# An encoder block in exact fp32 by halves: the gate projection's first products interleaved, tiles placed in another order, filler matmuls dealt out anew

## The chip, the cores and the metric

The kernel runs on one core of a Trainium2 chip. The metric is the device time of one execution in microseconds (us), the median over runs. A second figure, the span, is the length of one profiled execution as the hardware profiler shows it; that execution also has a time of its own.

## The reference

One layer of a hybrid bidirectional encoder: 1024 tokens, model width 1024, everything in float32.

```
h = RMSNorm(x)
q,k,v,r, lr_f,lr_b, sq,sk,sv, gate_a,gate_b = split(h @ W_in)
A = bidirectional gated linear attention(q,k,v; gates from lr_f, lr_b), 4 heads,
    chunked, per-head RMSNorm, times silu(r), then @ W_oA
B = windowed attention (+-128 tokens, blocks of 128), 8 query heads, 2 key heads,
    QK-norm, rotary positions, a sink logit per head, then @ W_oB
x = x + (sigmoid(gate_a) * A + sigmoid(gate_b) * B) @ W_out
x = x + SwiGLU(RMSNorm(x))
```

## The kernel before, in words

Every large product works on 128x128 blocks of weights against 128x512 blocks of activations. A float32 operand is split into a high part in TensorE's reduced float32 format (ScalarE's copy, `h`) and the remainder (VectorE's subtraction, `l`); a product is the sum of three matmuls, high x high, high x low and low x high. `wunit` is the helper for a weight block of 128x512: a load on the SP queue into `wr`, the split into `wh` (L70) and `wl` (L72). A result stays in a PSUM bank (`mmtile`, four banks, or `chtile`, four more) until ScalarE or VectorE copies it out.

The kernel goes through these stages.

1. Head of the kernel: x is loaded in blocks `xr[k, s]` (k = 0 to 7 blocks of 128 features, s = 0, 1 halves of the tokens), split, and used for the first head's q and k and for the low-rank gate codes `lr`.
2. The branch gates `gate_a`, `gate_b`, eight pairs f = 0 to 7. Each pair is computed with seven block products instead of eight (a Strassen-like scheme on 2x2 blocks: features in two halves, tokens in two halves). `x_first(f)` does the first two of the seven: one product into a bank, ScalarE's copy `p1` out of it (L320), a second product added in the same bank, and a copy and store of the sum (`keep_raw`). After the first pair, the RMS statistics (`acc`, 20 small matmuls, `rstd`) follow. `xcombos(k, step)` builds the combinations T1 to T4 of x blocks on ScalarE and VectorE. `x_two`, `x_four` and `x_last` do the remaining five products of each pair. Their results are stored and fetched again later. The halves of x that the combinations overwrote are read again (`x_load`) and split again during pair 7.
3. Gated linear attention (GLA). First the gate codes and their weights are loaded into a staging pool `ip` (`upr`, `lrf`), scaled and split into `lrS` and `upS` (L444 to L455). Then 45 slots t = 0 to 44 follow; in each, up to six steps of different (head, chunk) pairs: `g_gates`, `g_scores`, `g_out`, `g_back_out`, `g_turn`.
4. Windowed attention (SWA), 22 slots (the last has no step): `k_prep`, `a_prep`, `a_scores`, `a_turn`, `k_turn`, `a_out`, `a_probs`.
5. The branches: `prep_a(s)` loads, for k = 0 to 7, an attention output (`lo`) and an r block (`lr`) through two buffers each, forms o * gain * r * sigmoid(r) and splits it into `oah`, `oal` (L899, L900). `branch_a` multiplies with W_oA in groups of 24 matmuls, eight inputs deep; `prep_b`, `branch_b` do the same for the other attention, and `out_proj` follows.
6. The feed-forward network in the same seven-product scheme, from about 1093 us to the end.

**Filler.** The projections for v, the other heads' q and k, SWA's inputs and r0 to r7 are kept as Python generators in the list `dense`, each step one matmul: five of 192 and fourteen of 48. `fill(n)` issues the next n. In GLA and SWA, `slot(stages, n)` issues the slot's steps in turn and spreads n filler matmuls behind them; a slot without a step deals none. `need(key)` issues 12 at a time until a projection that a step reads has been computed. At the end of SWA, `fill(1 << 30)` issues what is left, after the last slot with a step (slot 20).

**Order.** On TensorE the order is the program's own (`manual_schedule`). On the other engines and on the SP queue, which issues all loads and stores, a planner at build time sorts the instructions by readiness in its own model of time; each queue then runs its list in order. A tile in a pool lies at a fixed place; pools are stacked, and a new pool lies where closed pools were, so the first writer of a new tile waits until the last reader of the old ones is done.

**Places.** In the gates' stage the stack is `ep` (e0 to e3 and two buffers `c`), `x0` (all sixteen x blocks), `w0`, `t0`. In GLA's, over the same place, it is `gc` (`lrS`, `upS`, `mask`, `tri`: 10.5 KB per partition), `stgA` (four buffers of 2 KB for filler results), `ip` (8 KB), and after `ip` is closed `gt` in its place. The seven products' results reuse x tiles: `p1` of pairs 0 to 3 lies in e0 to e3, of pairs 4 to 7 in `xr01` to `xr31`; `c21` in `xr00`, `xr10`, `c22` in `xr20`, `xr30`.

Of the kernel before, what the change touches and what calls it, by code (L numbers as in the profile page):

```python
# [8 lines left out]
F32 = mybir.dt.float32  # L9
# [21 lines left out]
def body(tc, i, out):  # L31
    nc = tc.nc
    with ExitStack() as root:
# [8 lines left out]
        def nm(s):  # L42
            uid[0] += 1
            return f"{s}_{uid[0]}"

        def mmtile(shape=(P, 512), dt=F32):
            return psm.tile(list(shape), dt, tag="mm", name=nm("mm"))
# [18 lines left out]
        def wunit(src, n=512):  # L66
            raw = wp.tile([P, n], F32, tag="wr", name=nm("wr"), bufs=4)
            nc.sync.dma_start(out=raw, in_=src)
            h = wp.tile([P, n], FR, tag="wh", name=nm("wh"), bufs=5)
            nc.scalar.activation(h, raw, AF.Copy)  # L70
            l = wp.tile([P, n], FR, tag="wl", name=nm("wl"), bufs=5)
            nc.vector.tensor_tensor(l, raw, h.bitcast(F32), op=ALU.subtract)  # L72
            return h, l
# [152 lines left out]

        g0s = ExitStack()
        ep = g0s.enter_context(tc.tile_pool(name="ep", bufs=1))
        x0 = g0s.enter_context(tc.tile_pool(name="x0", bufs=1))
        w0 = g0s.enter_context(tc.tile_pool(name="w0", bufs=1))  # L230
        t0 = g0s.enter_context(tc.tile_pool(name="t0", bufs=1))
# [1 line left out]
        nc.vector.tensor_scalar(ng1, g1, -1.0, None, op0=ALU.mult)  # L233
        xr = {}

        def x_load(k, s, tag=None):
            t = x0.tile([P, HT], F32, tag=tag or f"xr{k}{s}", name=nm("xr"))
            nc.sync.dma_start(out=t, in_=i["xT"][k, s])
            return t

# [22 lines left out]
        def xcombos(k, step):  # L263

            b11, b12, b21, b22 = xr[k, 0], xr[k, 1], xr[k + 4, 0], xr[k + 4, 1]
            ga, nga, gb = g1[:, k:k + 1], ng1[:, k:k + 1], g1[:, k + 4:k + 5]
            if step == 0:
                nc.vector.tensor_tensor(b12, b12, b11, op=ALU.subtract)
                h = xp.tile([P, HT], FR, tag=f"xh{k}1", name=nm("T1h"))
                l = xp.tile([P, HT], FR, tag=f"xl{k}1", name=nm("T1l"))  # L270
                x_split(h, l, b12, ga)
                X0["T1"].append((h, l))
                nc.scalar.activation(b12, b12, AF.Copy, scale=ga)
                nc.vector.scalar_tensor_tensor(b22, b22, gb, b12, op0=ALU.mult, op1=ALU.subtract)
                xsplit("T2", k, b22)
            else:
                nc.vector.scalar_tensor_tensor(b11, b11, nga, b22, op0=ALU.mult, op1=ALU.add)
                xsplit("T3", k, b11)
                nc.vector.scalar_tensor_tensor(b21, b21, gb, b22, op0=ALU.mult, op1=ALU.subtract)
                xsplit("T4", k, b21)  # L280
# [13 lines left out]
        def product(o, w, x, nk, start, stop):  # L294
            h, l = w
            for kk in range(nk):
                c = slice(kk * P, (kk + 1) * P)
                nc.tensor.matmul(o, h[:, c], x[kk][0], start=start and kk == 0, stop=False, skip_group_check=True)  # L298
                nc.tensor.matmul(o, h[:, c], x[kk][1], start=False, stop=False, skip_group_check=True)  # L299
                nc.tensor.matmul(o, l[:, c], x[kk][0], start=False, stop=kk == nk - 1, skip_group_check=True)  # L300
# [6 lines left out]
        def keep_raw(name, s, b, n=P):  # L307
            c = ep.tile([P, HT], F32, tag="c", name=nm("c"), bufs=2)
            nc.scalar.copy(c[:n], b[:n])
            keep(name, s, c[:n])  # L310
# [1 line left out]
        pairs = [Chunk() for _ in range(NG)]  # L312

        def x_first(f):
            F = pairs[f]
            Y = mmtile()
            product(Y, wunit(i["w_f"][16 + f, 0]), X0["11"], 4, True, False)
            F.p1 = ep.tile([P, HT], F32, tag=f"e{f}", name=nm("xp1")) if f < 4 else \
                x0.tile([P, HT], F32, tag=f"xr{f - 4}1", name=nm("xp1"))
            nc.scalar.copy(F.p1, Y)  # L320
            product(Y, wunit(i["w_f"][16 + f, 1]), X0["21"], 4, False, True)
            keep_raw(f"ga{f}", 0, Y)

        def w0load(f, q):
            t = wp.tile([P, 512], F32, tag="wr", name=nm("wr"), bufs=4) if q % 10 == 1 else \
# [41 lines left out]

        with tc.manual_schedule(engines={mybir.EngineType.PE}):
            xr[0, 0] = x_load(0, 0)

            wu = chtile((P, 512))
            for _ in range(12):
                mm(wu[:, :P], ones, ones, True, True)
            bq = [[mmtile(), mmtile()] for _ in range(2)]
            us = [wunit(i["w_f"][m, 0]) for m in range(2)]
            xr[0, 1] = x_load(0, 1)
            for k in range(KT):
                if k < KT - 1:
                    for s in range(2):
                        xr[k + 1, s] = x_load(k + 1, s)  # L380
                if k == 4:
                    us = [wunit(i["w_f"][m, 1]) for m in range(2)]
                c = slice((k % 4) * P, (k % 4 + 1) * P)
                for s in range(2):
                    x_split(xh[k][s], xl[k][s], xr[k, s], g1[:, k:k + 1])
                    for m in range(2):
                        mm3(bq[m][s], us[m][0][:, c], us[m][1][:, c], xh[k][s], xl[k][s], k == 0, k == KT - 1)
            ident = load_const(cst, "ident", i["c_ident"], (P, P))
            g2 = load_const(cst, "g2", i["g2"], (P, KT))
            og = load_const(cst, "og", i["og"], (P, 2))  # L390
            bl = [chtile((P, 512)), chtile((P, 512))]
            for u in range(2):
                lr_mm(bl, u)
            for m in range(2):
                for s in range(2):
                    keep_raw(("q0", "k0")[m], s, bq[m][s])
            for s in range(2):
                keep_raw("lr", s, bl[s], 96)
            for k in range(KT):
                for s in range(2):  # L400
                    x_square(k, s)
            for f in range(NG):
                x_first(f)
                if f == 0:
                    for s in range(2):
                        v = chtile((P, HT))
                        mm(v, ones, acc[s], True, True)
                        rsqrt(rstd[:, s * HT:(s + 1) * HT], v, 1.0 / T, EPS, epst, w0, (P, HT), "", ("rsl", "rst"))
                    vt = chtile((P, KT, 2))
                    for t in range(KT):  # L410
                        mm(vt[:, t], acc[t // 4][:, (t % 4) * P:(t % 4 + 1) * P], ones[:, 0:2], True, True)
                    rsqrt(rstdt, vt[:, :, 0], 1.0 / T, EPS, epst, pad, (P, KT), "rt")
                for k in range(f, 4, 4):
                    xcombos(k, 0)
                for k in range(f - 4, 4, 4):
                    if f >= 4:
                        xcombos(k, 1)
            for f in range(NG):
                x_two(f)
                if f == NG - 1:  # L420
                    for k in range(4):
                        r = x_load(k, 1, f"xr{4 + k}0")
                        xh[k][1] = xp.tile([P, HT], FR, tag=f"xh{k}1", name=nm("xh"))
                        xl[k][1] = xp.tile([P, HT], FR, tag=f"xl{k}1", name=nm("xl"))
                        x_split(xh[k][1], xl[k][1], r, g1[:, k:k + 1])
                if f:
                    x_last(f - 1)
                x_four(f)
            x_last(NG - 1)
# [7 lines left out]
        nc.vector.memset(mask, 1.0)  # L437
        nc.vector.memset(mask[:, :, 0:1], 0.0)
        tri = load_const(gc, "tri", i["c_tri"], (P, P), U32)
        stg = glas.enter_context(tc.tile_pool(name="stgA", bufs=4))  # L440
        ini = ExitStack()
        ip = ini.enter_context(tc.tile_pool(name="ip", bufs=1))
        upr = ip.tile([98, 2, 512], F32, tag="upr", name="upr")
# [10 lines left out]
        nc.scalar.activation(lrS[0:96], lrf, AF.Copy)  # L454
        nc.vector.tensor_tensor(lrS[32:64], lrf[32:64], lrS[32:64].bitcast(F32), op=ALU.subtract)  # L455
        ini.close()

        gt = glas.enter_context(tc.tile_pool(name="gt", bufs=2))

# [189 lines left out]
        with tc.manual_schedule(engines={mybir.EngineType.PE}):  # L649
            fill(24)  # L650
            for t in range(last + 1):
                n = 40 if t < 6 else 26 if t < NH * NC + 3 else 12
                slot([(lambda v=at[t, j]: v[0](*v[1:])) if (t, j) in at else None for j in (0, 5, 4, 3, 2, 1)], n)
        glas.close()

# [176 lines left out]
        with tc.manual_schedule(engines={mybir.EngineType.PE}):  # L832
            for t, v in enumerate(todo):
                v.sort(key=lambda e: order.index(e[0]))
                slot([lambda e=e: e[0](*e[1:]) for e in v], 36 if t < 2 else 24 if t < 2 * KT + 2 else 8)
            fill(1 << 30)
        swas.close()
        xstack.close()
# [497 lines left out]
```

## Time and profile before

| | |
|---|---|
| median of 3 runs | 1724.73 us (1724.39 to 1727.88) |
| profiled execution | 1723.14 us, span 1721.4 us |
| busy: TensorE, VectorE, ScalarE | 1671.7, 1253.2, 909.9 us |
| mean granted TensorE clock | 0.99 |
| data moved | 251.89 MB, 146 GB/s |

Lines of the profile name engines as PE (TensorE's matmuls), PEld (its weight loads), DVE (VectorE), ACT (ScalarE), POOL and SPq (the SP queue's issue of a transfer). A row of waits reads: engine, tile and line that waited, who ended the wait, then the sum in us, the count, the longest. A row of the timeline reads: start in us, duration (of all of them, where a count stands at the end), engine, line, operation, output<-inputs, shapes, count, and in brackets the idle time before it with the releaser. A matmul's duration of 0.39 us overlaps the next one's; the distance of two starts is what it costs.

### The profile page before, as it was taken

The numbers are of one execution on the slowest core, as the hardware profiler recorded it, in microseconds if no ns is written. First come the engines' busy times: TensorE is split into PE (matmuls) and PEld (weight loads), VectorE is DVE, ScalarE is ACT, GpSimd is POOL, SyncE is SP. The second block draws the span as 40 slices with busy tenths as digits, with TensorE's granted clock in tenths as the row PEclk, the third lists the DMA queues.
The fourth block names the chain that finished last, engine by engine and source line by source line (L and its number), as shares of the span: only waits on it lengthen the run. The fifth ranks groups of instructions, "written<-read, shape, count | busy, mean of one in ns | idle before, by whom it ended". The sixth has DMA issues, their size and how long they took to land.

```text
span 1721.4 us, 23818 instructions
## 1 busy us (share of the span) xinstructions
PE 1671.7 (97%) x7808; PEld 1375.7 (80%) x7808; DVE 1253.2 (73%) x2591; ACT 909.9 (53%) x2017; POOL 0.2 (0%) x4
## 2 busy tenths in 40 slices
PE   9899989999999899997999999999999999999999
PEld 7678778888888778884788888788888888778887
DVE  8656566787885598765686468978777887779755
ACT  8422354687877699875454456633333333354442
POOL 0000000000000000000000000000000000000000
PEclk9999989999999999998899999999999999999999
DMA  7433443343544643226666555343333354396433
GB/s 235 147 115 131 134 129 103 111 130 119 148 120 132 186 133 100 87 74 214 207 206 193 169 148 174 108 155 120 105 104 128 135 174 144 116 349 207 134 111 117
DMA packets 157068, 251.89 MB, mean 146 GB/s; under 512 B 17966, under 2 KB 43438, under 8 KB 156944
## 3 DMA queue, kind: packets, MB, share of 16 engines
q1 hardware_dynamic: 156944, 250.37, 45.5%
q8 instruction: 61, 1.00, 0.2%
q14 instruction: 63, 0.52, 0.1%
HBM read 182.80 MB, written 67.50 MB: 145 GB/s over the span
## 4 chain that ended last, share of the span: by engine, by line
PE 73%; DVE 5%; ACT 4%; DMA 3%; issue 1%; SPq 0%; DVEq 0%; ACTq 0%
PE mm L76 30%; PE ch L76 7%; PE mm L1153 6%; PE mm L298 5%; PE mm L299 5%; PE mm L300 5%; PE ch L1153 5%; PE ch L299 2%; PE ch L298 2%; PE ch L300 2%; PE ch L801 1%; DMA lo<-o 1%; DMA ga<-ga 1%; DMA kvr<-skv 0%; DMA lr<-r 0%
## 5 line engine op out<-in xcount | busy, mean ns | idle before, releaser
L72 DVE TENSOR_TENSOR wl<-wr,wh 128x512 fp32r<-128x512 f32 (+1 forms) x240 | 164.0, 686 | 74.6 <-ACT wh L70 73.5
L70 ACT ACTIVATE wh<-wr 128x512 fp32r<-128x512 f32 (+1 forms) x240 | 150.0, 628 | 127.3 <-PE mm L76 84.8
L290 ACT ACTIVATE wh<-ws 128x512 fp32r<-128x512 f32 x120 | 76.0, 634 | 182.3 <-PE mm L299 85.6
L76 PE MATMUL mm<-wh,xh 128*128 128x512 f32 x320 | 128.7, 402 | 0.3 <-ACT st L186 0.3
L76 PE MATMUL mm<-wl,xh 128*128 128x512 f32 x320 | 127.8, 399 | 0.0
L76 PE MATMUL mm<-wh,xl 128*128 128x512 f32 x320 | 127.4, 398 | 0.0
L291 DVE TENSOR_TENSOR wl<-ws,wh 128x512 fp32r<-128x512 f32 x120 | 82.3, 686 | 29.2 <-ACT wh L290 29.1
L76 PE MATMUL mm<-xh,wh 128*128 128x512 f32 x256 | 102.8, 401 | 0.4 <-ACT wh L70 0.4
L76 PE MATMUL mm<-xl,wh 128*128 128x512 f32 x256 | 102.7, 401 | 0.1
L290 ACT ACTIVATE wh<-wr 128x512 fp32r<-128x512 f32 x60 | 38.0, 634 | 105.4 <-issue 49.6
L290 ACT ACTIVATE wh<-a 128x512 fp32r<-128x512 f32 x66 | 41.9, 635 | 89.3 <-PE ch L1153 42.2
L76 PE MATMUL mm<-xh,wl 128*128 128x512 f32 x256 | 85.3, 399 | 0.0
L291 DVE TENSOR_TENSOR wl<-a,wh 128x512 fp32r<-128x512 f32 x66 | 45.5, 690 | 42.0 <-ACT wh L290 41.6
L1153 PE MATMUL mm<-hh,wh 128*128 128x512 f32 x176 | 68.6, 390 | 1.3 <-ACT hh L1125 1.3
L76 PEld LDWEIGHTS mm<-wh,xh 128*128 128x128 f32 x320 | 60.9, 190 | 10.9 <-ACT st L186 1.0
L1153 PE MATMUL mm<-hl,wh 128*128 128x512 f32 x176 | 68.7, 390 | 1.0 <-DVE hl L1126 1.0
L76 PEld LDWEIGHTS mm<-wh,xl 128*128 128x128 f32 x320 | 60.8, 190 | 10.6
L76 PEld LDWEIGHTS mm<-wl,xh 128*128 128x128 f32 x320 | 60.8, 190 | 10.0
L1153 PE MATMUL mm<-hh,wl 128*128 128x512 f32 x176 | 68.6, 390 | 0.1
L76 PE MATMUL mm<-oah,wh 128*128 128x512 f32 x128 | 53.2, 416 | 10.3 <-ACT oah L899 10.1
L1126 DVE TENSOR_TENSOR hl<-hr,hh 128x512 fp32r<-128x512 f32 x77 | 52.7, 685 | 5.3 <-ACT hh L1125 5.3
L76 PEld LDWEIGHTS mm<-xh,wh 128*128 128x128 f32 x256 | 48.2, 188 | 7.7 <-ACT wh L70 0.5
(576 smaller groups left out, 4910.9 us busy)
## 6 DMA issues: line engine op xcount, KB each, us to landing
wr<-in_w_fi_dram SPq DMA_DIRECT2D x102, 256.0 KB, 2.8
wr<-in_w_f_dram SPq DMA_DIRECT2D x80, 256.0 KB, 2.8
wr<-in_w_t_dram SPq DMA_DIRECT2D x80, 256.0 KB, 2.8
B<-c SPq DMA_DIRECT2D x44, 256.0 KB, 2.1
T<-tx SPq DMA_DIRECT2D x44, 256.0 KB, 2.3
a<-in_w_fo_dram SPq DMA_DIRECT2D x44, 256.0 KB, 5.2
hr<-T SPq DMA_DIRECT2D x44, 256.0 KB, 2.6
hr<-B SPq DMA_DIRECT2D x33, 256.0 KB, 4.5
```

What stands on the lines that cost most here:

```text
L70: nc.scalar.activation(h, raw, AF.Copy)
L72: nc.vector.tensor_tensor(l, raw, h.bitcast(F32), op=ALU.subtract)
L76: nc.tensor.matmul(o, a, b, start=start, stop=stop)
L290: nc.scalar.activation(h, src, AF.Copy)
L291: nc.vector.tensor_tensor(l, src, h.bitcast(F32), op=ALU.subtract)
L298: nc.tensor.matmul(o, h[:, c], x[kk][0], start=start and kk == 0, stop=False, skip_group_check=True)
L299: nc.tensor.matmul(o, h[:, c], x[kk][1], start=False, stop=False, skip_group_check=True)
L300: nc.tensor.matmul(o, l[:, c], x[kk][0], start=False, stop=kk == nk - 1, skip_group_check=True)
L801: nc.tensor.transpose(pt[:, h], a.p[:, h, (kb - a.b0) * P:(kb - a.b0 + 1) * P], ident)
L1126: nc.vector.tensor_tensor(l, r, h.bitcast(F32), op=ALU.subtract)
L1153: nc.tensor.matmul(ys[m], a[:, c], b, start=f0, stop=f1, skip_group_check=True)
```

## The change

- `x_first` takes pairs f and f + 1 at once, with a bank each: first product of f, first product of f + 1, second product of f, second product of f + 1. The loop runs over f = 0, 2, 4, 6. The statistics come after the first two pairs, and `xcombos` is called for two blocks after each call.
- Four x tiles (`xr40`, `xr50`, `xr60`, `xr70`) move to a pool `xa` of their own between `ep` and `x0`. The re-read halves of x go to e0 to e3 instead of those four.
- `stgA` is opened after `ip` is closed, so that it takes the place of `ip`, and `ip` lies directly behind `gc`.
- The filler per slot: in GLA 36 instead of 40 for t < 6 and 24 instead of 26 up to t = 34; in SWA 56 instead of 36 in the first two slots, 22 instead of 24 up to slot 17, and 6 instead of 8 after that.

```diff
+        xa = g0s.enter_context(tc.tile_pool(name="xa", bufs=1))
         x0 = g0s.enter_context(tc.tile_pool(name="x0", bufs=1))
...
-        def x_load(k, s, tag=None):
-            t = x0.tile([P, HT], F32, tag=tag or f"xr{k}{s}", name=nm("xr"))
+        def x_load(k, s, again=False):
+            t = ep.tile([P, HT], F32, tag=f"e{k}", name=nm("xr")) if again else \
+                (xa if k > 3 and s == 0 else x0).tile([P, HT], F32, tag=f"xr{k}{s}", name=nm("xr"))
...
         def x_first(f):
-            F = pairs[f]
-            Y = mmtile()
-            product(Y, wunit(i["w_f"][16 + f, 0]), X0["11"], 4, True, False)
-            F.p1 = ep.tile(...) if f < 4 else x0.tile(...)
-            nc.scalar.copy(F.p1, Y)
-            product(Y, wunit(i["w_f"][16 + f, 1]), X0["21"], 4, False, True)
-            keep_raw(f"ga{f}", 0, Y)
+            Y = [mmtile(), mmtile()]
+            for j in range(2):
+                F = pairs[f + j]
+                product(Y[j], wunit(i["w_f"][16 + f + j, 0]), X0["11"], 4, True, False)
+                F.p1 = ep.tile(...) if f < 4 else x0.tile(...)
+                nc.scalar.copy(F.p1, Y[j])
+            for j in range(2):
+                product(Y[j], wunit(i["w_f"][16 + f + j, 1]), X0["21"], 4, False, True)
+                keep_raw(f"ga{f + j}", 0, Y[j])
...
-            for f in range(NG):
+            for f in range(0, NG, 2):
                 x_first(f)
...
-                for k in range(f, 4, 4):
-                    xcombos(k, 0)
-                for k in range(f - 4, 4, 4):
-                    if f >= 4:
-                        xcombos(k, 1)
+                for k in range(2):
+                    xcombos(f % 4 + k, f // 4)
...
-                        r = x_load(k, 1, f"xr{4 + k}0")
+                        r = x_load(k, 1, True)
...
-        stg = glas.enter_context(tc.tile_pool(name="stgA", bufs=4))
         ini = ExitStack()
...
         ini.close()
+        stg = glas.enter_context(tc.tile_pool(name="stgA", bufs=4))
...
-                n = 40 if t < 6 else 26 if t < NH * NC + 3 else 12
+                n = 36 if t < 6 else 24 if t < NH * NC + 3 else 12
...
-                slot([...], 36 if t < 2 else 24 if t < 2 * KT + 2 else 8)
+                slot([...], 56 if t < 2 else 22 if t < 2 * KT + 2 else 6)
```

More of the change, by code (lines that the diff above doesn't have):

```diff
@@ L314, in x_first @@
         def x_first(f):
-            F = pairs[f]
-            Y = mmtile()
-            product(Y, wunit(i["w_f"][16 + f, 0]), X0["11"], 4, True, False)
-            F.p1 = ep.tile([P, HT], F32, tag=f"e{f}", name=nm("xp1")) if f < 4 else \
-                x0.tile([P, HT], F32, tag=f"xr{f - 4}1", name=nm("xp1"))
-            nc.scalar.copy(F.p1, Y)
-            product(Y, wunit(i["w_f"][16 + f, 1]), X0["21"], 4, False, True)
-            keep_raw(f"ga{f}", 0, Y)
+            Y = [mmtile(), mmtile()]
+            for j in range(2):
+                F = pairs[f + j]
+                product(Y[j], wunit(i["w_f"][16 + f + j, 0]), X0["11"], 4, True, False)
+                F.p1 = ep.tile([P, HT], F32, tag=f"e{f + j}", name=nm("xp1")) if f < 4 else \
+                    x0.tile([P, HT], F32, tag=f"xr{f + j - 4}1", name=nm("xp1"))
+                nc.scalar.copy(F.p1, Y[j])
+            for j in range(2):
+                product(Y[j], wunit(i["w_f"][16 + f + j, 1]), X0["21"], 4, False, True)
+                keep_raw(f"ga{f + j}", 0, Y[j])
         def w0load(f, q):
@@ L834, in body @@
                 v.sort(key=lambda e: order.index(e[0]))
-                slot([lambda e=e: e[0](*e[1:]) for e in v], 36 if t < 2 else 24 if t < 2 * KT + 2 else 8)
+                slot([lambda e=e: e[0](*e[1:]) for e in v], 56 if t < 2 else 22 if t < 2 * KT + 2 else 6)
             fill(1 << 30)
```

## The prediction

> **What bounds the kernel now.** I read the page's head and engine rows first, then the waits of TensorE, then one row per stage from the busy time by stretch, and last the timeline around each long wait.
>
> ```profile
> span 1721.4 us, 23818 instructions
> PE 1671.7 (97%) x7808; PEld 1375.7 (80%) x7808; DVE 1253.2 (73%) x2591; ACT 909.9 (53%) x2017; POOL 0.2 (0%) x4
> PE mm L76 <- ACT oah L899: 10.1, 7, 3.4
> PE mm L298 <- ACT xp L320: 8.0, 8, 1.2
> PE ch L76 <- DVE lrS L455: 7.6, 1, 7.6
> PE ch L626 <- ACT ob L620: 2.3, 1, 2.3
> PE ch L726 <- DVE qn L704: 2.0, 1, 2.0
> ```
>
> TensorE (PE) is the bound: 49.7 us without a matmul in 1721.4. The waits name where: the first projection through the attention branch's input (L899), the copies of the gates' first products (L320), and the one wait for the gate codes (L455). The edit touches these places and changes no matmul's shape or number, so it can gain only what PE loses, and the row of a stage says how much that is.
>
> ```profile
> 39.90:100.10 60.20, 52.18 (x225) 40.22 (x224) 33.92 (x56) 27.15 (x52) 0.00 (x0) 1.00 0.43 138
> 140.00:160.00 20.00, 20.00 (x90) 16.58 (x89) 13.03 (x21) 5.35 (x9) 0.00 (x0) 1.00 0.38 128
> 212.90:227.00 14.10, 6.45 (x19) 5.15 (x19) 9.02 (x18) 6.59 (x9) 0.00 (x0) 0.64 0.37 102
> 230.00:573.00 343.00, 338.70 (x1856) 287.66 (x1855) 246.33 (x666) 238.75 (x638) 0.00 (x0) 1.00 0.42 127
> 573.60:786.70 213.10, 204.80 (x1059) 169.11 (x1058) 160.26 (x566) 172.03 (x543) 0.00 (x0) 1.00 0.35 111
> 640.00:660.00 20.00, 20.00 (x112) 17.23 (x110) 19.56 (x72) 19.96 (x68) 0.00 (x0) 1.00 0.43 132
> 786.70:826.30 39.60, 28.31 (x79) 16.79 (x78) 26.11 (x41) 17.94 (x29) 0.00 (x0) 0.71 0.80 255
> ```
>
> Columns: stretch, its length, busy time (count) of PE, weight load, DVE, ACT, POOL, granted clock, DMA share, GB/s. Rows 1 to 7: the pairs' first products; the next stage, where PE never pauses; start of linear attention (GLA); GLA; window attention (SWA); its saturated part, where DVE and ACT have no idle time left; the passage into the branches. Row 2 gives the pitch of a 512-column matmul: 20/90, which the timeline below refines to 0.227 us (23 steps from 207.30 to 212.51).
>
> **Term A, first products in turn.** Now each pair runs 12 matmuls into a bank, waits for ScalarE's copy out of it, then adds 12 more.
>
> ```profile
> 42.41 0.39 PE L300 MATMUL mm<-xh,wl 128*128 128x512 f32 x1
> 44.04 0.50 PE L298 MATMUL mm<-xh,wh 128*128 128x512 f32 x1 [1.25 <-ACT xp L320]
> 52.96 0.39 PE L300 MATMUL mm<-xh,wl 128*128 128x512 f32 x1
> 53.70 0.57 ACT L320 COPY xp<-mm 128x512 f32<-128x512 f32 x1
> 54.32 0.50 PE L298 MATMUL mm<-xh,wh 128*128 128x512 f32 x1 [0.97 <-ACT xp L320]
> ```
>
> Start to start is 1.36 us where 0.227 would do: 1.13 lost, in seven of eight pairs, and 1.40 in the first (1.63 - 0.23). Sum 9.3. The restart costs 0.1 more each (0.34 to the second matmul). With two banks, the other pair's 12 matmuls (2.72 us) lie between a product and its successor, against 1.36 for the copy. I take **-9.5**; ends -10.2 and -6 (no loss: the same 192 matmuls, with a wait less on the way). What could be late next: the weights, since a 256 KB unit is now used each 2.72 us, not 3.35. Row 2 has that rate with every unit split and combined, so it holds. Moved with this: the second product's load on the SP queue, its split, the copy and the store, each by 12 matmuls, with two spare banks behind; the 20 statistics matmuls after the first pair, 24 matmuls (5.4 us) later, and rstd with them, hidden since its first user, the gate codes, comes 150 us later; the combinations of blocks 1 and 3, earlier by one pair on DVE and ACT (34 and 27 us busy in 60), needed only in the next stage.
>
> **Term B, places of tiles.** The codes' staging pool now lies where the codes are loaded after pair 7's last products are stored:
>
> ```profile
> 208.22 0.32 SPq L304 DMA_DIRECT2D gb<-xc  x1
> 210.39 0.39 SPq L444 DMA_DIRECT2D upr<-in_up_dram  x1
> 218.19 1.06 ACT L454 ACTIVATE lrS<-lrf 96x1024 fp32r<-96x1024 f32 x1
> 219.28 1.22 DVE L455 TENSOR_TENSOR lrS<-lrf,lrS 32x1024 fp32r<-32x1024 f32 x1 [1.48 <-ACT lrS L454]
> 207.30 0.39 PE L76 MATMUL mm<-wh,xh 128*128 128x512 f32 x1
> 212.51 0.39 PE L76 MATMUL mm<-wh,xl 128*128 128x512 f32 x1
> 220.55 0.80 PE L76 MATMUL ch<-lrS,upS 98*128 98x256 f32 x2 [7.65 <-DVE lrS L455]
> 221.15 0.63 PE L76 MATMUL mm<-wh,xh 128*128 128x512 f32 x1
> 225.84 0.59 PE L76 MATMUL mm<-wh,xl 128*128 128x512 f32 x1
> ```
>
> From load to codes takes 10 us; PE has 24 filler matmuls (5.4 us) for it. After the change the staging sits on the constants' neighbours, the ep pool's 12 KB and the four second-half tiles of x, read for the last time in the pairs' first stage, 100 us earlier; the codes themselves take e0 to e3, free once the re-read x halves are split (about 197). So the chain can end before 212.7 and the 7.65 us go. So do the 12 matmuls at pitch (225.84 - 221.15)/11 = 0.426: 12 x 0.20 = 2.4. **-10.1**; ends -10.1 and 0 (the load still late in its queue; later than now it cannot be, since all that it waits for is read before pair 7's last store). [...] Moved here: four re-reads of x (SP queue) now wait for pair 3's last product instead of an x tile; pairs 4 to 7 lie between, and PE reads them only in the next projections. The stores' tiles (stgA) now wait for the staging; the first is written 78 filler matmuls in. If that cover fails, it costs the remainder of the 10 us.
>
> **Term C, GLA filler.** Filler is 1632 matmuls (5 x 192 + 14 x 48), dealt out by slot. Following the loops (slots 1 and 43 have no stage and deal none; a forced need deals 24 now, 48 after), GLA has 24 + 5x40 + 29x26 + 9x12 + 24 = 1110 now and 24 + 5x36 + 29x24 + 9x12 + 48 = 1056 after. 54 fewer, x 0.227 = 12.2 us, if PE still sets the slot. Row 4 says it does: 4.3 idle in 343, 2.3 of it one wait at the end, while DVE is at 72% and ACT at 70%. The same DVE and ACT work in 331 us instead of 343 is 74% and 72%; I allow 1.2 of new waits. **-11**; ends -12.2 and -5. Forced needs: v0 waits in slot 2, 12 matmuls, but its user in slot 3 stands 30 matmuls behind it, not 26; k1 in slot 8 is awaited at the same count of 300.
>
> **Term D, SWA filler.** To its last output product it deals 472 now (1582 - 1110), 476 after (1532 - 1056): +0.9. The first two slots get 20 more each, which hides the 2.0 for qn. In slots 2 to 17, two fewer save 0.45 each only where PE is the bound; in about five slots of row 6's kind they save nothing: +2.3. **+1**; ends -3 (the early slots let DVE and ACT run ahead) and +5.
>
> **Term E, the passage.** Now 50 filler matmuls follow the last output product, then branch a waits for its inputs.
>
> ```profile
> 786.51 0.39 PE L76 MATMUL ch<-ph,vSl 128*128 128x512 f32 x1
> 797.67 0.61 PE L76 MATMUL mm<-xh,wl 128*128 128x512 f32 x2
> 790.96 0.32 SPq L907 DMA_DIRECT2D lo<-o  x1
> 797.05 0.69 DVE L912 TENSOR_TENSOR lr<-lr,sg 128x512 f32<-128x512 f32 x1 [3.26 <-DMA ga<-ga]
> 798.98 1.28 DVE L125 TENSOR_TENSOR st<-mm,rstd 128x512 f32<-128x512 f32 x2
> 800.18 0.74 DVE L913 SCALAR_TENSOR_TENSOR lo<-lo,og,lr 128x512 f32<-128x512 f32 x1
> 802.04 0.69 DVE L900 TENSOR_TENSOR oal<-lo,oah 128x512 fp32r<-128x512 f32 x1
> 819.00 2.64 DMA lr<-r
> 819.55 0.61 ACT L911 ACTIVATE sg<-lr 128x512 f32<-128x512 f32 x1
> 823.00 0.68 DVE L900 TENSOR_TENSOR oal<-lo,oah 128x512 fp32r<-128x512 f32 x1
> 824.76 0.63 PE L76 MATMUL mm<-oah,wh 128*128 128x512 f32 x1
> ```
>
> From t = 786.74 (end of that product) to branch a's second group are 38.0 us for 16.8 us of matmuls (74 x 0.227). The inputs set it: the first is ready at 802.7, the eighth at 823.7, 3.0 us each through two buffers. After, 100 matmuls stand there (94 left over and 6 of slot 20), 22.7 us of cover. The inputs' work already starts under cover (797.05 is before the filler's end at 798.1), and only the first waits behind r7's evacuation (798.98). Without that its second step starts at 797.7, and 2.55 us later (802.73 - 800.18) it is ready, at 800.3 or t+13.6, and the eighth at t+34.5. r7 itself comes at t+22.7 + 1.3 (evacuation) + 2.2 (store, as 208.22 to 210.39) + 2.6 (load) + 4.1 (819.55 to 823.68) = t+33: just not later. So **-2.4**. Ends: -9.9 (PE-bound: 22.7 + 5.4 = 28.1) and +11.4 (everything behind r7, whose end is 50 x 0.227 later).
>
> **Sum.** -9.5 - 10.1 - 11 + 1 - 2.4 = -32.0. The profiled execution took 1723.14, 1.74 over its span, and 1.59 under the median of the runs, 1724.73; so 1691.1 for such an execution and 1692.7 for the median, which I predict as 1693. About 0.2% (3.4 us) is what a measurement of this kernel can tell from no change.
>
> **Rivals.** (1) The inputs wait behind r7: DVE or SP issue in a fixed order, and if r7's evacuation or store stands ahead of the inputs' work, E is +11.4: 1706.5. For it: 798.98 stands ahead of the first input's second step. Against: 797.05 got in front. (2) The codes come late all the same (queue order, not space): B is 0, 1702.8. For it: the SP queue carries stores and weights then; against: the load at 210.39 follows a store's landing. (3) Thin slots show the chains: with C at -5 and D at +5, 1702.7. For it: row 6; against: row 4. (4) Slower: in the slots the weight splits (ACT, then DVE) fall behind the attention's own work, and PE waits for its filler in every slot. It decides from 32.0/45 = 0.71 us per GLA slot, 1725 and above. Against: the whole of GLA now has 4.3 us idle; 0.45 less per slot is the most that could appear as a wait if nothing else gets longer.
>
> **How the numbers follow.** Forecast 0.62, its own range 1684 to 1698; (1) 0.10; (2) 0.09; (3) 0.13; (4) 0.03; several terms failing together, no change, 0.03. Faster 0.94, same 0.03, slower 0.03. Low end: D and E at their better ends (-4.0 and -7.5), 1681; high end: rivals 1 to 3 one at a time, 1707.
>
> **What would show it.** A: no wait for L320, the stage's 24 matmuls in 5.44 us. B: the load of upr before 207, no wait for lrS, clock 1.00 there. C: a GLA about 11 shorter from the first gate product on, and its PE idle under 6. D: no wait for qn; more idle PE around the saturated slots. E: first input ready before the filler ends, waits for L899 of about 2 each for the last three or four inputs, and 35 us from the last output product to the second group. The prediction is wrong if L899's waits stay at 10 us, if lrS still holds PE, or if new waits for splits appear in the slots.

## The result and the profile after

| | before | after |
|---|---|---|
| median of the runs, us | 1726.06 (4 runs, 1724.39 to 1727.88) | 1699.92 (4 runs, 1698.4 to 1701.4) |
| span of the profiled execution, us | 1721.4 | 1696.6 |

The ratio of the times is 0.9848, 95% interval 0.9831 to 0.9865: 26 us faster. The prediction said 1693, in a range of 1681 to 1707. The page of the kernel after, head, TensorE's row and its clock:

```profile
span 1696.6 us, 23838 instructions
PE 1666.8 (98%) x7808; PEld 1375.7 (81%) x7808; DVE 1252.3 (74%) x2591; ACT 905.7 (53%) x2017; POOL 0.2 (0%) x4
PEclk9999999999999999998999999999999999999999
```

TensorE is still the bound, with 29.8 us without a matmul instead of 49.7. Of its waits in the kernel after, those that the argument needs (line, what it waited for, us in total, times, longest):

```profile
PE mm L76 <- ACT oah L901: 4.8, 5, 1.4
PE ch L803 <- DVE sql L757: 3.6, 2, 3.0
PE ch L76 <- ACT ph L806: 2.5, 1, 2.5
PE ch L76 <- DVE mx L771: 1.9, 8, 0.5
PE ch L76 <- ACT vh L539: 1.4, 1, 1.4
PE ch L628 <- ACT ob L622: 0.6, 1, 0.6
```

The 8.0 us for the copies of the first products and the 7.6 for the codes are gone, and the inputs of branch a cost 4.8 instead of 10.1. New inside the window attention (SWA) is the wait for sql, and there is more of mx (1.2 before) and ph (2.1 before).

To see where the time went, I cut every kernel at the same six places: the first gate product, the first product of the next stage, the first product of the gate codes (start of GLA), the last transpose of `g_turn` (its end), the last output product of SWA, and branch a's second group (its 25th matmul). Microseconds from the timeline:

| | first products | on to the codes | GLA | SWA | passage | to the end | span |
|---|---|---|---|---|---|---|---|
| before | 57.5 | 123.2 | 352.8 | 213.2 | 38.3 | 896.6 | 1721.4 |
| after | 47.1 | 116.0 | 338.8 | 219.5 | 39.3 | 896.0 | 1696.6 |
| difference | -10.4 | -7.2 | -14.0 | +6.3 | +1.0 | -0.6 | -24.8 |

The stretch of GLA starts at the codes, so it holds both term C and the second piece of term B, the half clock behind the codes (0.50 from 216.02 to 226.26 us in the kernel before).

The sums of busy time by stretch for GLA, SWA and the passage, with these ends, before:

```profile
220.55:573.35 352.80, 348.50 (x1888) 295.55 (x1888) 253.81 (x685) 244.05 (x648) 0.00 (x0) 0.99 0.41 126
573.35:786.51 213.16, 204.86 (x1061) 169.17 (x1059) 160.26 (x566) 172.19 (x543) 0.00 (x0) 1.00 0.35 111
786.51:824.76 38.25, 26.96 (x77) 15.73 (x76) 24.81 (x38) 16.98 (x28) 0.00 (x0) 0.72 0.79 255
```

and after, with the first products and the start of GLA ahead of them:

```profile
40.00:87.00 47.00, 47.00 (x213) 38.54 (x212) 32.95 (x55) 25.71 (x49) 0.00 (x0) 1.00 0.45 140
200.00:206.50 6.50, 6.50 (x32) 5.39 (x30) 2.34 (x5) 1.75 (x3) 0.00 (x0) 1.00 0.74 226
203.06:541.88 338.82, 335.02 (x1841) 284.05 (x1840) 249.37 (x681) 236.85 (x642) 0.00 (x0) 1.00 0.43 127
541.88:761.36 219.48, 208.11 (x1059) 169.51 (x1058) 162.51 (x567) 174.91 (x547) 0.00 (x0) 0.99 0.36 111
761.36:800.63 39.27, 33.23 (x126) 24.13 (x125) 26.39 (x41) 17.62 (x30) 0.00 (x0) 0.89 0.80 262
```

The reader is to see three things. In the first two rows after, PE has no pause and the full clock. GLA is shorter mainly because it holds fewer matmuls (1841 records against 1888). SWA holds as many records of matmuls as before (1059 against 1061), but PE is idle for 11.4 us in it instead of 8.3, and its busy time is 3.2 us longer: something makes it wait and then run slowly.

### The profile page after: what moved, and what is told of

The parts are those of the page before. It is cut to its first block, busy times and chain, and to the rows that moved or that the text cites. A ratio compares the mean times of both kernels' runs of the same rounds, so it can differ in the third digit from the quotient of the medians.

```text
span 1696.6 us, 23838 instructions
## 1 busy us (share of the span) xinstructions
PE 1666.8 (98%) x7808; PEld 1375.7 (81%) x7808; DVE 1252.3 (74%) x2591; ACT 905.7 (53%) x2017; POOL 0.2 (0%) x4
## 4 chain that ended last, share of the span: by engine, by line
PE 84%; DVE 6%; ACT 5%; DMA 4%; issue 1%; SPq 0%; ACTq 0%; DVEq 0%
PE mm L76 30%; PE mm L300 8%; PE mm L301 8%; PE mm L302 8%; PE ch L76 7%; PE mm L1155 7%; PE ch L1155 5%; PE ch L300 3%; PE ch L301 3%; PE ch L302 3%; ACT p L786 1%; DVE wl L72 1%; PE ch L803 1%; ACT p L792 1%; DMA lo<-o 1%
## 5 line engine op out<-in xcount | busy, mean ns | idle before, releaser
L292 ACT ACTIVATE wh<-wr 128x512 fp32r<-128x512 f32 x60 | 37.9, 632 | 105.4 <-issue 49.6
L76 PEld LDWEIGHTS mm<-xl,wh 128*128 128x128 f32 x256 | 48.5, 189 | 7.4 <-DVE xl L245 0.8
```

What stands on the lines that cost most here:

```text
L76: nc.tensor.matmul(o, a, b, start=start, stop=stop)
L292: nc.scalar.activation(h, src, AF.Copy)
```

## The experiments

Every kernel is compared with the kernel before on the same chip; times are medians. The first three take one part of the change each.

**e1, first products in turn, alone**: the kernel before, with `x_first` and `xcombos` as in the change.

```diff
...
-            for f in range(NG):
+            for f in range(0, NG, 2):
                 x_first(f)
...
```

> The kernel before with the first products in turn alone (and the statistics and combinations that move with them). Theory (the terms add up by stage): the pairs' first stage shortens by 10.3 us, as between the two profiles (57.5 to 47.1), nothing else moves, 1716 us against 1726. Rival (the gain is given back at the next wait, since the codes' chain and the attention slots start from the same queues): less than 7 us.

1715.08 us, ratio 0.9945 (0.9932 to 0.9957). The stage took 47.1 us, exactly as in the kernel after, 10.4 less; SWA took 1.2 more than before. Term A stands.

**e2, places of tiles, alone**: the kernel before, with the pools of the x tiles and the order of `stgA` and `ip` as in the change.

```diff
...
-                        r = x_load(k, 1, f"xr{4 + k}0")
+                        r = x_load(k, 1, True)
...
-        stg = glas.enter_context(tc.tile_pool(name="stgA", bufs=4))
...
         ini.close()
+        stg = glas.enter_context(tc.tile_pool(name="stgA", bufs=4))
```

> The kernel before with the places of tiles alone (pool xa, the re-read halves in e0 to e3, stgA behind ip). Theory: the wait for lrS and the half-clock matmuls behind it go, 7.2 + 2.4 = 9.6 us, 1716 us. Rival (queue order, not space, delays the codes when the first products keep their order): 3 us or less, and a wait for lrS stays.

1718.99 us, 0.9968 (0.9956 to 0.9981). The codes are in time (116.4 us instead of 123.2 up to them, -6.8), but only 5.5 us of the 9.6 expected arrive. The row of GLA and two waits of this kernel:

```profile
214.00:566.00 352.00, 346.27 (x1888) 293.61 (x1887) 253.91 (x686) 243.66 (x649) 0.00 (x0) 1.00 0.42 128
```
```profile
PE mm L76 <- ACT oah L901: 12.1, 7, 4.9
PE ch L728 <- DVE qn L706: 1.7, 1, 1.7
```

The half clock is gone from GLA (granted clock 1.00, 0.99 before), and its busy time falls by 2.2 us (348.50 to 346.27), as the second piece of B said; but its idle time rises by 1.4 (4.3 to 5.7), so that GLA gains 0.8. In this execution another 3.4 us were lost in SWA (+1.2) and in the passage (+2.2), whose input waits rose from 10.1 to 12.1; why is open.

**e3, filler, alone**: the kernel before with the new counts.

```diff
-                n = 40 if t < 6 else 26 if t < NH * NC + 3 else 12
+                n = 36 if t < 6 else 24 if t < NH * NC + 3 else 12
...
-                slot([...], 36 if t < 2 else 24 if t < 2 * KT + 2 else 8)
+                slot([...], 56 if t < 2 else 22 if t < 2 * KT + 2 else 6)
```

> The kernel before with the new filler counts alone. Theory: linear attention 11.6 us shorter, windowed attention 6.3 longer, the passage 1.0 longer, in sum -4.3, 1722 us. Rival (the planner's order of the other engines' work, not the counts, made the windowed stage longer in the profile after): windowed stage within 2 us of 213, and a sum of -9 or better.

1718.82 us, 0.9967 (0.9954 to 0.9979). GLA and SWA of this kernel:

```profile
220.21:558.97 338.76, 336.63 (x1840) 285.71 (x1840) 248.92 (x680) 236.06 (x641) 0.00 (x0) 0.99 0.41 126
558.97:777.48 218.51, 207.63 (x1058) 169.64 (x1057) 162.23 (x567) 174.87 (x547) 0.00 (x0) 0.99 0.36 112
```

GLA alone gives the whole 14.0 us: 11.9 less busy, 2.2 less idle. SWA gives back 5.4 of them. So most of the loss in SWA belongs to the counts, those of GLA and SWA together; with the counts of before, e1 and e2 lengthen SWA by 1.2 each.

**e4, SWA's counts as before, the rest as after.**

```diff
-                slot([...], 56 if t < 2 else 22 if t < 2 * KT + 2 else 6)
+                slot([...], 36 if t < 2 else 24 if t < 2 * KT + 2 else 8)
```

> The changed kernel with the old counts in windowed attention (36, 24, 8), so that 96 matmuls instead of 94 are left for its end. Theory (the new counts there cost their 6.3 us): windowed stage back to about 213 us, passage unchanged, 1694 us against 1700. Rival (accident of order): windowed stage stays near 219, 1700 us. Second rival (the stage needs the early filler to hide its loads, which shows only now that linear attention ends sooner): a wait for qn of 2 us or more returns and the gain is 3 us or less.

1698.41 us, 0.9851 (0.9836 to 0.9866): against the kernel after, no difference that can be told. SWA took 216.2, 3.3 less than after, but still 3.0 more than before; GLA and the passage took 1.2 and 1.1 more. The wait at SWA's start came back, 2.9 us, now put down to issue and not to qn. The second rival had expected that and a small gain, but the lag that the wait leaves is soon made up. Counted from GLA's end, the transposes of `a_turn` start 3.3 us later than in the kernel before in slot 2, 0.5 earlier in slot 4, and 0.1, 1.5 and 2.3 later in slots 7, 11 and 17. So the 3.0 build up in the later slots, and why these are longer stays open. Undoing all counts at once hides what each does, so the next two kernels keep one half each.

**e5, only the early slots fuller** (56, 24, 8; 38 matmuls fewer left over), and **e6, only the late slots thinner** (36, 22, 6; 40 more left over).

```diff
-                slot([...], 56 if t < 2 else 22 if t < 2 * KT + 2 else 6)
+                slot([...], 56 if t < 2 else 24 if t < 2 * KT + 2 else 8)
```
```diff
-                slot([...], 56 if t < 2 else 22 if t < 2 * KT + 2 else 6)
+                slot([...], 36 if t < 2 else 22 if t < 2 * KT + 2 else 6)
```

> The changed kernel with the late slots of the sliding-window stage back at 24 and 8 and only the two early slots at 56: the stage deals 520 matmuls where the changed kernel deals 482, so 38 fewer are left over for the stage's end. Theory (the early surplus is paid in full, because TensorE then runs ahead of VectorE and ScalarE and waits for them): the stage is longer than the 216.2 us of the run with 36, 24 and 8 by the 40 early matmuls at 0.227 us, 9.1 us, so 225 us, with the wait for sql (L757) of about 3 us as in the changed kernel; the leftover is shorter by 8.6 us, the passage takes back what it does not need as cover, and the span ends 0 to 2 us above the changed kernel's: about 1700 to 1702 us in all. Rival (the thin late slots expose the two other engines, and the early filler is harmless): the stage is about 222 us at most, the wait for sql is gone, and the time is 1695 to 1698.

> The changed kernel with the early slots of the sliding-window stage back at 36 and the late ones left at 22 and 6: the stage deals 442 matmuls. Theory (the thin slots are not exposed, only the early surplus cost): the stage shortens from 216.2 us, that of the run with 36, 24 and 8, by 38 matmuls at 0.227 us, 8.6 us, to about 207.6 us; the wait for sql (L757) is absent; the 40 matmuls come back in front of the branches, so the time is that of the run with 36, 24 and 8 or up to 1 us below, 1697 to 1698.5. Rival (thin slots expose VectorE and ScalarE): the stage stays at 211 us or longer, waits of TensorE for ph (L806), mx (L771) and sql (L757) sum to over 4 us more, and the time is 1701 to 1704.

e5: 1702.38 us, 0.9869 (0.9852 to 0.9885). e6: 1701.01 us, 0.9860 (0.9843 to 0.9877). SWA's row in e4, in e5 and in e6:

```profile
542.46:758.64 216.18, 207.13 (x1055) 169.83 (x1054) 161.06 (x567) 173.73 (x547) 0.00 (x0) 0.98 0.36 113
```
```profile
542.12:764.25 222.13, 214.56 (x1094) 178.19 (x1093) 165.08 (x571) 175.76 (x549) 0.00 (x0) 0.98 0.36 115
```
```profile
541.34:753.83 212.49, 199.62 (x1018) 163.58 (x1017) 159.93 (x566) 174.00 (x546) 0.00 (x0) 0.98 0.36 111
```

Up to its last output product, e5 deals 40 matmuls more than e4, 9.1 us, and SWA is 6.0 longer: busy +7.4, idle -1.5. e6 deals 36 fewer there, 8.2 us, and SWA is 3.7 shorter: busy -7.5, idle +3.8 (9.1 to 12.9). Neither theory holds alone. By these rows, an early matmul costs two thirds of its time; a late one that is taken away gives less than half of it. In e6 the waits that grew are for pl, VectorE's remainder of the probabilities (3.3 us, 0.4 in e4), and for sob, ScalarE's copy of the output (1.2), not those that the rival named. And its surplus at the end is not free either: the passage of e6 takes 47.3 us against 40.3 in e4, with one wait of 8.5 for the eighth input of branch a.

In the kernel after, both losses stand together: 216.2 + 6.0 - 3.7 = 218.5, measured 219.5. But these are single executions: with the same counts and the same code up to there, SWA took 222.0 and 221.1 in e7 and e10 below, so each of the two prices is good to 2 or 3 us. How it looks, in the kernel after (a stretch of 10 us, ScalarE's part of the split of the queries and two matmuls in it):

```profile
601.88:611.88 10.00, 7.48 (x33) 6.26 (x34) 6.69 (x24) 9.98 (x38) 0.00 (x0) 0.83 0.27 80
```
```profile
602.61 0.60 ACT L756 ACTIVATE sqh<-ch 128x512 fp32r<-128x512 f32 x1
604.08 0.90 PE L803 MATMUL ch<-ident,p 128*128 128x128 f32 x4 [2.98 <-DVE sql L757]
606.92 0.78 PE L76 MATMUL mm<-xh,wh 128*128 128x512 f32 x1
```

At equal slots counted from GLA's end, the kernel after was 7.6 us later than the kernel before in slot 2 (it had dealt 33 more matmuls since), caught up to 3.0 by slot 5, and then fell back to 7.4 in slot 6. ScalarE is busy for all of these 10 us and comes to sqh only at 602.61; VectorE's sql follows, and PE, which is ahead, waits 2.98 us for it. Behind the wait PE runs slowly: the granted clock is 0.83 over the 10 us, and a matmul takes 0.78 us whose record is 0.39 at full clock.

**e7, three buffers for the branches' inputs, else as after**, and **e8, the same with SWA's counts of e4**.

```diff
+LB = 3
...
-                o = btile("lo")
+                o = btile("lo", bufs=LB)
...
-                r = btile("lr")
+                r = btile("lr", bufs=LB)
...
-            g = btile(nme[:2])
+            g = btile("g")
```

> The changed kernel with three buffers instead of two for the branches' inputs lo and lr; to make room the tiles ga and gb share one name and its two buffers. Theory (the passage into the branches is paced by the loop of two buffers, load, product, load into the same buffer, with the loads taking over 4 us while r7 is evacuated): the inputs become ready at under 3.0 us each instead of 3.34, the waits for oah (L901, 4.8 us) fall below 2 us, the passage goes from 39.3 to about 36 us, and the time to 1696 or 1697. Rival (the inputs are paced by VectorE's and ScalarE's own work on them, or by the transfer itself): the passage stays within 0.7 us of 39.3 and the time within 1 us of the changed kernel's.

> The changed kernel with both: three buffers for lo and lr (ga and gb sharing two) and the sliding-window stage's counts back at 36, 24 and 8. By the theory on the two-buffer loop its passage, 40.3 us with two buffers and 6.6 us of waits for oah (L901), goes to about 36.5, and the time from 1698.4 to 1694 or 1695. By the rival (VectorE, ScalarE or the transfer sets the pace) it stays at 1698.

e7: 1696.46 us, 0.9841 (0.9826 to 0.9856); the passage took 37.9, 1.3 less than after, between the two theories' figures, and the longest input wait was 4.0; its interval and that of the kernel after overlap. e8: 1693.68 us, 0.9821 (0.9806 to 0.9835), 0.3% under e4, and the passage 37.6 instead of 40.3. The first seven inputs came at 2.50 us each on average (772.01 to 787.02); the eighth came 6.5 us after the seventh. The last steps in e8 (VectorE's scaling of r7, SP's store, SP's load, ScalarE's first use, PE):

```profile
781.48 1.29 DVE L126 TENSOR_TENSOR st<-mm,rstd 128x512 f32<-128x512 f32 x2
782.20 0.92 SPq L127 DMA_DIRECT2D r<-st  x2
786.01 0.32 SPq L912 DMA_DIRECT2D lr<-r  x1
790.41 0.63 ACT L914 ACTIVATE sg<-lr 128x512 f32<-128x512 f32 x1 [3.85 <-DMA lr<-r]
793.45 0.79 PE L77 MATMUL mm<-oah,wh 128*128 128x512 f32 x1 [4.96 <-ACT oah L902]
```

The last filler matmul started at 781.28. Its result is scaled and stored, the load of it is issued 3.8 us after the store, ScalarE uses it 4.4 later: the eighth input is r7 itself, come back from memory.

**e10, r7 by halves, else as after**, and **e9, the same on e8**. The last projection of the filler computes 48 matmuls for the first half of the tokens, stores them, then the other 48; the number of matmuls is the same.

```diff
-                  proj_t("sq1", 4)] + [proj_f(f"r{m}", 8 + m) for m in range(8)]
+                  proj_t("sq1", 4)] + [proj_f(f"r{m}", 8 + m) for m in range(7)] + [proj_h("r7", 15)]
...
+        def proj_h(name, m):
...
+                us = [next_unit(), next_unit()]
+                for s in range(2):
+                    for k in range(KT):
+                        h, l = us[k // 4]
...
+                    nc.sync.dma_start(out=d, in_=t)
+                    scr[name, s] = d
```

> The changed kernel with one thing more: r7, the last projection of the filler, is computed by halves of the columns (48 matmuls for the first half, its result stored, then 48 for the second) instead of both halves together. Theory (with 88 matmuls left over it is r7's own way out and back, the last filler product, its scaling on VectorE, the store, the load into lr, that brings the eighth input of branch a; it was ready 14.6 us after the filler's end): r7's first half is stored some 10 us earlier, the eighth input no longer waits for it, the passage falls from 39.3 us to what the loop of two buffers allows, 14.6 + 7 x 3.0 + 2 = 37.6, and the time by 1 to 2 us, to 1698. Rival (the two-buffer loop or VectorE sets the whole pace, r7 comes in any case): the passage stays within 0.7 us of 39.3 and the time at 1700.

> The kernel with three buffers for lo and lr and the sliding-window counts 36, 24 and 8, and with r7 by halves as well. Theory (r7's round trip is the last bound there: the eighth input is ready 12.5 us after the filler's end, after a wait of ScalarE of 3.9 us for the load of lr): the eighth input is ready when the loop of three buffers brings it, 14.6 + 7 x 2.5 = 32 us after the stage's last product, the passage falls from 37.6 us to about 34, and the time from 1693.7 to 1690 or 1691. Rival (the inputs are late for another cause, the transfers as such): the passage stays at 37 or more, the time at 1693 to 1694.

e10: 1701.69 us, 0.9871 (0.9856 to 0.9886); the passage took 39.3, as after. e9: 1690.07 us, 0.9802 (0.9789 to 0.9815); the passage took 34.9. The waits for the last inputs in e9, and its passage's row:

```profile
789.79 0.50 PE L77 MATMUL mm<-oah,wh 128*128 128x512 f32 x1 [2.02 <-ACT oah L923]
```
```profile
756.72:791.61 34.89, 31.10 (x130) 24.32 (x129) 25.18 (x40) 18.14 (x30) 0.00 (x0) 0.98 0.84 277
```

Two bounds lie on top of each other in the passage, the loop of two buffers and r7's way through memory. With SWA's counts of the kernel after, halving r7 alone gives nothing (39.3) and three buffers alone give 1.3. With the counts of before, three buffers alone give 2.7 and both give 5.4 (40.3 in e4, 34.9 here). The halves alone with those counts were not run.

**e11, e9 with 28 instead of 36 matmuls in each of the two early slots.**

> As the kernel before it in this call, with the two early slots of the sliding-window stage at 28 instead of 36, so that 16 more matmuls (3.6 us) are left over for the passage. Theory (an early matmul is paid at 6.0 of 9.1 us, two thirds, and the passage has idle room once r7 no longer holds it): the stage is 2.4 us shorter, the passage no longer, and the time 1 to 2.5 us below that kernel's, 1688 to 1690. Rival (the early slots' chains are exposed when the filler is cut below 36, as the thin late slots were): the stage is less than 1 us shorter and the time the same or up to 1.5 us above.

1687.37 us, 0.9787 (0.9774 to 0.9800), the fastest version: 0.6% under the kernel after. SWA and the passage, and PE at SWA's start:

```profile
541.16:752.97 211.81, 201.31 (x1039) 167.78 (x1037) 161.49 (x567) 172.71 (x547) 0.00 (x0) 0.98 0.36 114
752.97:789.57 36.60, 33.92 (x146) 27.50 (x145) 24.77 (x40) 17.57 (x29) 0.00 (x0) 0.97 0.79 253
```
```profile
558.89 0.66 PE L750 MATMUL ch<-ident,qn 128*128 128x128 f32 x2 [6.61 <-issue]
559.77 0.63 PE L77 MATMUL mm<-wh,xl 128*128 128x512 f32 x1
561.48 0.63 PE L77 MATMUL mm<-wh,xh 128*128 128x512 f32 x1
```

SWA is 4.3 us shorter than in e9 for 16 matmuls fewer (3.6), the passage 1.7 longer. So here the early matmuls were paid in full, not by two thirds. PE waits for 6.6 us once at the start (2.8 in e9), for something that the profile doesn't name, and its other waits in SWA fall from 6.4 to 3.9. The transposes of slot 2 start as late as in e9 (3.3 against 3.1 us behind the kernel before), so the filler that stood there in e9 only filled the wait. The wait that the change set out to fill was cheaper left empty.

## Why the prediction was right, and where its steps were not

The sign and the places were right, and the size roughly. The time came out 6.9 us above the forecast, inside the stated range but 1.9 above the forecast's own range of 1684 to 1698. The mechanism held for A and for the waits of B; B's second piece and C held in sum only, and D and E failed. That the sum is no further off is luck in part: D and E missed by 5.3 and 3.4 us, and 1.5 came back elsewhere. None of the four rivals took place as written, though (3) has a part in D and (1) in E. Of the signs of being wrong that the prediction named, one is there in part: a new wait for a split in the slots, for sql, which is the attention's own operand and no weight as in rival (4).

- **A, -9.5 forecast, -10.4 measured** (after and e1). No wait for L320 is left and the stretch has no pause. The pauses of 9.3 and eight restarts at 0.1 make 10.1; the -9.5 left most of the restarts out, and the measured time is just beyond the end of -10.2.
- **B, -10.1 forecast.** The first piece, 7.65, came as 7.2 (e2: 6.8). The codes are ready 5.3 us early in the kernel after:

```profile
186.71 0.46 SPq L445 DMA_DIRECT2D upr<-in_up_dram  x1
196.52 1.22 DVE L456 TENSOR_TENSOR lrS<-lrf,lrS 32x1024 fp32r<-32x1024 f32 x1
203.06 0.40 PE L76 MATMUL ch<-lrS,upS 98*128 98x256 f32 x2
```

  The second piece, 2.4 for the half clock, is there as busy time (2.2 in e2), but most of it was lost again as idle time in the same stage: only 0.8 of it shortened GLA. A wait for vh (L539), which the kernel before does not have, is 1.2 us in e2 and 1.4 in the kernel after; I did not test whether it is the whole of it.
- **C, -11 forecast, -14.0 measured in e3**, with the wait for the codes still there. In the kernel after, GLA is also 14.0 shorter, with B's second piece in it: 13.4 was forecast for the two. So the places of tiles added nothing to what the counts gave alone. The step that failed is the 1.2 us allowed for new waits, where the bound of -12.2 had excluded any gain: in e3 GLA's idle time fell by 2.2 instead, most of it the wait for ob at its end, 2.3 before and 0.6 in e3 and after. The stretch also holds 48 matmuls fewer, not the 54 of the count. In e3 and after, six filler matmuls that by the program's slots follow GLA's last transposes stand ahead of them (ten instead of four between the last product with `thb` and the transpose that waits for ob); they cover 1.4 us of that wait. Why they stand there the record doesn't show.
- **D, +1 forecast, +6.3 measured**, beyond the end of +5. The step that failed is the price: the prediction netted 40 early against 36 late matmuls at the same 0.227 us. The runs show other prices: early ones cost 6.0 of 9.1, late ones gave 3.7 of 8.2 (e5, e6). The remaining 3.0 stand in e4, where SWA has the counts of before and is longer all the same, in its later slots; their cause stays open. That the fuller early slots hide the wait for qn came true, and was worth less than they cost.
- **E, -2.4 forecast, +1.0 measured.** The filler ended at 784.3, 22.7 us behind the last output product, as forecast, and the first input was ready 14.6 us behind it instead of 13.6. The step that failed is the pace: "the eighth at t+34.5" kept 3.0 us per input, but it was 3.3 (775.53 to 798.87, seven steps, of which the one to the fourth input is 5.48). The loads of lr took longer than before, and r7's scaling stands ahead of the fourth input's split on VectorE. The DMA issues in the passage before, then after (KB each, median us to landing):

```profile
lr<-r SPq DMA_DIRECT2D x10, 256.0 KB, 2.8
```
```profile
lr<-r SPq DMA_DIRECT2D x10, 256.0 KB, 3.7
```
```profile
786.53 1.28 DVE L125 TENSOR_TENSOR st<-mm,rstd 128x512 f32<-128x512 f32 x2
787.73 0.68 DVE L902 TENSOR_TENSOR oal<-lo,oah 128x512 fp32r<-128x512 f32 x1
798.87 0.69 DVE L902 TENSOR_TENSOR oal<-lo,oah 128x512 fp32r<-128x512 f32 x1 [0.69 <-ACT oah L901]
```

  So rival (1) is there for one input, by the 1.2 us of the scaling, not for all at 11.4. "r7 itself comes at t+33: just not later" was right for the kernel after (e10 gains nothing by bringing it earlier), and it was the next bound, as e8 and e9 show. Its round trip in e8 was 12.7 us from the end of the last filler matmul (781.5) to the end of the eighth input's split (794.2), not the 10.2 forecast, because store and load took 3.8 and 4.4 us instead of 2.2 and 2.6.

The 50 extra matmuls in front of the branches (100 instead of 50) therefore covered what they should, while the inputs came later by nearly as much: the passage has 5.3 us less idle time (11.3 to 6.0) and is 1.0 us longer.

## What to carry to other kernels

A filler matmul has no single price: price it in the stage that takes it, by what the engines beside PE do there, because one that lets PE run ahead into a busy ScalarE is paid for two thirds or more (6.0 of 9.1 us in e5, 4.3 for 3.6 in e11) and one that is taken out of a saturated slot leaves a hole (e6: 8.2 us of matmuls fewer, 3.8 more idle). When filler is moved to cover a wait for data, ask what the last filler produces and who needs it, and follow it through memory and back; if two bounds lie on top of each other (here the buffers and the round trip), lifting one alone shows nothing or a part of the gain, and they must be lifted together.

## What the runs showed of the hardware

PE ran slowly not only behind the long wait for the codes (7.65 us in the kernel before). The granted clock in the traces of the kernels before and after is 1.00 or 0.50. Up to the last product it is 0.50 in five stretches: 216.02 to 226.26 (10.24 us) and 803.11 to 827.00 (23.89) in the kernel before; 604.29 to 607.71 (3.41), 792.02 to 802.26 (10.24) and 1481.52 to 1484.93 (3.41) in the kernel after. 10.24 and 23.89 are three and seven times 3.41. In e11 such a stretch lies at 555.39 to 562.22 (6.83; the clock is 0.71 over 551.16 to 561.16 and 0.95 over the next 10 us). Busy time and clock in the 3.41 us ahead of a stretch at 0.50 and in it, first in the kernel before, at the wait for the codes:

```profile
212.61:216.02 3.41, 0.29 (x2) 0.00 (x0) 1.54 (x3) 1.69 (x2) 0.00 (x0) 1.00 0.97 258
216.02:226.26 10.24, 5.71 (x14) 4.56 (x15) 6.83 (x14) 4.23 (x6) 0.00 (x0) 0.50 0.21 64
```

Then in the kernel after, at the passage's end, with one of the matmuls there (the first one after the wait of 1.00 us at 790.20 has 0.50 us at full clock):

```profile
788.61:792.02 3.41, 1.82 (x5) 0.64 (x5) 3.33 (x6) 1.38 (x3) 0.00 (x0) 1.00 0.93 297
792.02:802.26 10.24, 7.27 (x13) 4.02 (x14) 7.09 (x12) 4.96 (x9) 0.00 (x0) 0.50 0.89 297
793.03 0.80 PE L76 MATMUL mm<-oah,wh 128*128 128x512 f32 x1 [1.36 <-ACT oah L901]
```

Here PE was not idle throughout ahead of the stretch: 1.59 us of the 3.41 had no matmul, and in the stretch at 0.50 waits of 1.0 to 1.4 us have three matmuls between them. Ahead of the five stretches, 3.41 us held 3.12 and 2.59 us without a matmul in the kernel before, and 2.98, 1.59 and 1.87 in the kernel after. The last 3.41 us of each, before the clock is 1.00 again, held 0.00 and 0.02, and 0.32, 0.04 and 0.21. Idle time of much the same length was not followed by 0.50 everywhere: in the kernel after, 1.77 us without a matmul in 751.06 to 754.48 and the wait for vh (1.40 us, to 226.48) were followed by 1.00. What makes the difference was not shown.
